# Feed-forward up-projection: 48 of 88 tile pairs as seven block products (Strassen), weights' low halves by accumulating DMA, five parts for three

## The chip, the cores and the metric

One core of one Trainium2 chip runs the whole program in one launch. The metric is device time in microseconds (us), from one run of the program; lower is better. The engines are named as in the profile: PE (TensorE, the matmuls), PEld (its weight loads), DVE (VectorE), ACT (ScalarE), POOL (GpSimd) and SP (SyncE, which here issues DMAs). Each engine works through its own list of instructions in order, and an instruction that waits for a semaphore holds up all that stands behind it in the same list.

## The reference, cut to what matters

Four layers with different token mixers; each is followed by the same kind of gated feed-forward block with a three-tap convolution along the tokens. D is 1024, D_FF is 2816, and there are 128 context tokens and 512 latent tokens, 640 in all. Modulation vectors (shift, scale, gate) come from a product of a conditioning vector with `ada_w` for each layer.

```python
def conv3_centred(x, w):
    xp = jnp.pad(x, ((0, 0), (1, 1), (0, 0)))
    return xp[:, :-2] * w[0] + xp[:, 1:-1] * w[1] + xp[:, 2:] * w[2]

def conv_ffn(h, w_up, conv_w, w_down):
    a = conv3_centred(h @ w_up, conv_w)          # h: tokens x 1024, w_up: 1024 x 5632
    g, u = a[..., :D_FF], a[..., D_FF:]
    return (jax.nn.silu(g) * u) @ w_down         # w_down: 2816 x 1024

# in reference(), for each layer l, and alike for the context tokens (xp, mod_p):
    mod_s = (jax.nn.silu(c) @ ada_w[l] + ada_b[l])[:, None, :]
    sh1s, sc1s, g1s, sh2s, sc2s, g2s = jnp.split(mod_s, 6, axis=-1)
...
    hs = modulate(xs, norm_ffn_g[l], sh2s, sc2s)
    xs = xs + g2s * conv_ffn(hs, ffn_w_up[l], ffn_conv[l], ffn_w_down[l])
```

## The kernel before

**Products.** Everything is kept feature by token: a tile has 128 features on the partitions and the 640 tokens as columns. Each f32 value is split into a high and a low part, and `mm3` makes each product as three matmuls: high by high, high by low, low by high. A matmul covers 320 columns. An up-projection tile has 8 k-tiles of 128 features, two halves of 320 columns and 3 matmuls for each, so 48 matmuls (`pe_half`, `proj`).

**The feed-forward block** (`ffn`) takes 22 pairs f of tiles for each layer: tile m = 2f is the g side, m = 2f + 1 the u side. They go in three parts of 8, 7 and 7 pairs (`PARTS`). In each part all up tiles come first ("up"), then their share of the down-projection ("dn"): 8 output tiles with 6 matmuls for each pair of the part. After the matmuls of an up tile, `post` has ACT scale it into c (L616), DVE add the two outer taps by four operations that read the PSUM tile (L618 and L620, each with 127 and with 511 columns), ACT take the silu of the g side (L633), POOL or, for the last pairs of a part, DVE multiply g by u (L640, L625), ACT cast the high part (L593) and POOL or DVE subtract for the low part (L594). dn starts on the pairs that are ready; its last needs the last pair's low part. DVE adds each dn tile into the residual x (L585).

**Weights.** SP loads a whole f32 chunk of 128x1024 into a "raw" tile; `pump1` splits it: ACT casts the high half (L86), DVE or POOL subtracts for the low half (L87). Five split tiles are kept at once.

**Modulation of the next layers** (`Ada`) is made in the shadow of the feed-forward blocks of layers 0 to 2: 144 chunks of 128x1024, a whole one at each step from a ring of tiles. For each, DVE takes a product with a sum (L209), POOL a second product (L214) and ACT the sum of that one (L215).

**Order.** The order in each engine's list is that in which the Python code calls the instructions; the waits between engines come from the tiles that they read and write, a whole tile at a time. PSUM has three double-bank tiles (`new_pair`) and two single ones.

Of the kernel before, what the change touches and what calls it, by code (L numbers as in the profile page):

```python
# [23 lines left out]
PARTS = ((0, 8), (8, 7), (15, 7))  # L24
# [27 lines left out]
class Weights:  # L52


    def __init__(self, g, chunks, slots):
        self.g, self.chunks, self.slots = g, chunks, slots
        self.loaded = self.split_n = self.used = 0
        self.raw, self.tiles = {}, {}
        self.cap = len(chunks)
        self.ahead = 2  # L60

    def load(self):
        i = self.loaded
# [12 lines left out]
    def pump1(self, pool=False):  # L76
        nc = self.g.nc
        i = self.split_n
        if i >= min(len(self.chunks), self.used + self.slots, self.cap):
            return  # L80
        while self.loaded <= i:
            self.load()
        n = self.chunks[i][1]
        raw = self.raw.pop(i)
        w = self.g.wp.tile([128, 2, 1024], F32R, tag="w", name=f"w{i}")
        nc.scalar.copy(w[:, 0, :n], raw[:, :n])  # L86
        (nc.gpsimd if pool else nc.vector).tensor_tensor(out=w[:, 1, :n], in0=raw[:, :n], in1=w[:, 0, :n], op=ALU.subtract)  # L87
        self.tiles[i] = w
        self.split_n += 1
        while self.loaded < min(self.split_n + self.ahead, len(self.chunks), self.cap):  # L90
            self.load()

    def take(self):
        while self.split_n <= self.used:
            self.pump()
        w = self.tiles.pop(self.used)
        self.used += 1
        return w


class Ada:
# [7 lines left out]
    def __init__(self, g):  # L109
# [21 lines left out]
    def micro(self):  # L131
# [15 lines left out]
        else:  # L147
            V.tensor_tensor_reduce(out=t if v else g.junk, in0=t, in1=g.cb[:, v, c], scale=1.0, scalar=0.0, op0=ALU.mult, op1=ALU.add,
# [10 lines left out]
        if self.ring is None:  # L159
            self.late.append(self.load) if self.late else self.load()  # L160

    def group(self, l, i):
# [8 lines left out]
        if self.ring is not None:  # L171
            V.memset(g.part[:, 1], 0.0)

    def open(self):

        self.ring = self.g.quad.tile([128, 5, 1024], F32, tag="quad", name=f"adaq{self.pos}")
        self.stop = len(self.queue)
        self.fresh = True
        self.pool = False
        self.hold = False  # L180
        self.flush()

    def begin(self):
        self.fresh = False
        while self.raw:
            self.micro()
        f = self.queue[self.pos][2] if self.pos < len(self.queue) else 0
        self.g.nc.vector.memset(self.g.part[:, 1, f:], 0.0)
        self.ring_load()

    def ring_load(self):
        while self.loaded < min(self.pos + 2, self.stop):
            l, i, f = self.queue[self.loaded]
            self.g.nc.sync.dma_start(out=self.ring[:, self.loaded % 3], in_=self.g.io["ada_t"][l - 1, i, f])
            self.loaded += 1

    def step(self):
        self.flush()
        if self.fresh:
            self.begin()  # L200
            return
        if self.pos >= self.stop:
            return
        g, nc = self.g, self.g.nc
        l, i, f = self.queue[self.pos]
        t, p0, p1 = self.ring[:, self.pos % 3], self.ring[:, 3], self.ring[:, 4]
        acc = g.part[:, 0, f]
        if g.mix:
            nc.vector.tensor_tensor_reduce(out=p0, in0=t, in1=g.cb[:, 0], scale=1.0, scalar=0.0, op0=ALU.mult, op1=ALU.add,  # L209
                                           accum_out=acc[:, 0:1])  # L210
        else:
            nc.gpsimd.tensor_tensor(out=p0, in0=t, in1=g.cb[:, 0], op=ALU.mult)
            self.late.append(lambda: nc.scalar.activation(p0, p0, AF.Copy, accum_out=acc[:, 0:1]))
        nc.gpsimd.tensor_tensor(out=p1, in0=t, in1=g.cb[:, 1], op=ALU.mult)  # L214
        self.late.append(lambda: nc.scalar.activation(p1, p1, AF.Copy, accum_out=acc[:, 1:2]))  # L215
        if f == KT - 1:
            self.late.append(lambda: self.group(l, i))
        self.pos += 1
        self.ring_load()

    def close(self):
        self.stop = self.loaded
        while self.pos < self.stop:
            self.step()
        self.flush()
        self.ring = None
# [1199 lines left out]
```

## Time and profile before

| | |
|---|---|
| median of 3 runs | 2717.39 us (2713.14 to 2717.69) |
| the profiled execution: own time | 2715.74 us |
| its span, first to last instruction | 2714.0 us |
| PE busy | 2675.2 us (99% of the span) |
| DVE, ACT, POOL busy | 1724.2, 1051.1, 859.0 us |
| a feed-forward part of 7 pairs, layer 1: up, then dn | 98.5 and 49.3 us |

The busy share of PE counts pipelined matmuls whose ends overlap, so a matmul's mean duration (309 ns) is longer than the distance between two. The distance is read from a stage: its length over its matmuls.

### The profile page before, as it was taken

The numbers are of one execution on the slowest core, as the hardware profiler recorded it, in microseconds if no ns is written. First come the engines' busy times: TensorE is split into PE (matmuls) and PEld (weight loads), VectorE is DVE, ScalarE is ACT, GpSimd is POOL, SyncE is SP. The second block draws the span as 40 slices with busy tenths as digits, with TensorE's granted clock in tenths as the row PEclk, the third lists the DMA queues.
The fourth block names the chain that finished last, engine by engine and source line by source line (L and its number), as shares of the span: only waits on it lengthen the run. The fifth ranks groups of instructions, "written<-read, shape, count | busy, mean of one in ns | idle before, by whom it ended". The sixth has DMA issues, their size and how long they took to land.

```text
span 2714.0 us, 45487 instructions
## 1 busy us (share of the span) xinstructions
PE 2675.2 (99%) x18950; PEld 2608.6 (96%) x18950; DVE 1724.2 (64%) x2623; ACT 1051.1 (39%) x1684; POOL 859.0 (32%) x442
## 2 busy tenths in 40 slices
PE   8999999999999999999999999999999999999998
PEld 6767999999999999999999999999999999999998
DVE  6454685868854378596866435958688548444344
ACT  4455453334442254243434224434344435223232
POOL 1223173445410144363521002635454115211121
PEclk9999999999999999999999999999999999999999
DMA  7233253334322233343322222433343123222221
GB/s 260 88 106 113 86 180 116 140 110 156 116 78 81 79 106 134 133 143 130 137 97 78 70 71 79 163 117 138 124 148 116 42 69 131 80 70 65 87 68 46
DMA packets 88335, 295.35 MB, mean 109 GB/s; under 512 B 9665, under 2 KB 15553, under 8 KB 88129
## 3 DMA queue, kind: packets, MB, share of 16 engines
q1 hardware_dynamic: 87554, 292.19, 32.0%
q8 instruction: 149, 2.44, 0.4%
q14 instruction: 56, 0.46, 0.1%
q10 hardware_dynamic: 576, 0.26, 0.0%
HBM read 289.53 MB, written 2.88 MB: 108 GB/s over the span
## 4 chain that ended last, share of the span: by engine, by line
PE 94%; DVE 2%; issue 2%; ACT 1%; DMA 0%; POOL 0%; SPq 0%; POOLq 0%; DVEq 0%; ACTq 0%
PE up L492 15%; PE up L493 15%; PE up L494 15%; PE dn L494 7%; PE dn L492 7%; PE dn L493 7%; PE sc L493 2%; PE sc L492 2%; PE sc L494 2%; PE S L774 1%; PE O L853 1%; PE qkv L492 1%; PE T L830 1%; PE sco L492 1%; PE fno L492 1%
## 5 line engine op out<-in xcount | busy, mean ns | idle before, releaser
L492 PE MATMUL up<-h,w 128*128 128x320 f32 x2816 | 871.4, 309 | 0.0
L494 PE MATMUL up<-h,w 128*128 128x320 f32 x2816 | 870.2, 309 | 0.0
L493 PE MATMUL up<-h,w 128*128 128x320 f32 x2816 | 870.1, 309 | 0.0
L87 DVE TENSOR_TENSOR w<-raw,w 128x1024 fp32r<-128x1024 f32 (+2 forms) x280 | 491.3, 1758 | 109.5 <-ACT w L86 102.0
L492 PEld LDWEIGHTS up<-h,w 128*128 128x128 f32 x2816 | 528.6, 188 | 0.3
L493 PEld LDWEIGHTS up<-h,w 128*128 128x128 f32 x2816 | 528.6, 188 | 0.3
L494 PEld LDWEIGHTS up<-h,w 128*128 128x128 f32 x2816 | 528.5, 188 | 0.0
L214 POOL TENSOR_TENSOR adaq<-adaq,cb 128x1024 f32<-128x1024 f32 x144 | 364.1, 2529 | 369.0 <-ACT adaq L215 320.2
L86 ACT CAST w<-raw 128x1024 fp32r<-128x1024 f32 (+2 forms) x361 | 363.9, 1011 | 240.3 <-PE dn L494 162.1
L492 PE MATMUL dn<-g,w 128*128 128x320 f32 x1408 | 436.3, 310 | 0.0
L494 PE MATMUL dn<-g,w 128*128 128x320 f32 x1408 | 435.1, 309 | 0.0
L493 PE MATMUL dn<-g,w 128*128 128x320 f32 x1408 | 435.1, 309 | 0.0
L87 POOL TENSOR_TENSOR w<-raw,w 128x1024 fp32r<-128x1024 f32 (+2 forms) x81 | 186.9, 2309 | 769.9 <-ACT w L86 647.6
L616 ACT ACTIVATE c<-up,fcv 128x640 f32<-128x640 f32 x176 | 140.1, 796 | 606.4 <-PE up L494 602.6
L618 DVE SCALAR_TENSOR_TENSOR c<-up,fcv,c 128x127 f32<-128x127 f32 x352 | 191.5, 544 | 230.2 <-ACT c L616 229.6
L209 DVE CUSTOM_DVE_ANT_0 adaq<-adaq,cb 128x1024 f32<-128x1024 f32 x144 | 268.8, 1867 | 0.1
L493 PEld LDWEIGHTS dn<-g,w 128*128 128x128 f32 x1408 | 264.3, 188 | 0.3
L492 PEld LDWEIGHTS dn<-g,w 128*128 128x128 f32 x1408 | 264.3, 188 | 0.3
L494 PEld LDWEIGHTS dn<-g,w 128*128 128x128 f32 x1408 | 264.3, 188 | 0.0
L585 DVE SCALAR_TENSOR_TENSOR x<-dn,mod,x 128x128 f32<-128x128 f32 (+3 forms) x204 | 99.4, 527 | 246.6 <-PE dn L494 246.5
L620 DVE SCALAR_TENSOR_TENSOR c<-up,fcv,c 128x127 f32<-128x127 f32 x352 | 193.6, 550 | 12.4
L640 POOL TENSOR_TENSOR c<-c,c 128x640 f32<-128x640 f32 x64 | 149.6, 2337 | 163.2 <-DVE c L620 158.4
(236 smaller groups left out, 3854.7 us busy)
## 6 DMA issues: line engine op xcount, KB each, us to landing
raw<-up SPq DMA_DIRECT2D x176, 512.0 KB, 4.2
adaq<-ada_t SPq DMA_DIRECT2D x144, 512.0 KB, 3.6
raw<-down SPq DMA_DIRECT2D x64, 448.0 KB, 3.9
adar<-ada SPq DMA_DIRECT2D x32, 512.0 KB, 3.6
raw<-down SPq DMA_DIRECT2D x32, 512.0 KB, 4.0
raw<-sc_in SPq DMA_DIRECT2D x24, 512.0 KB, 3.5
ada<-ada SPq DMA_DIRECT2D x16, 512.0 KB, 10.2
raw<-sgu_in SPq DMA_DIRECT2D x16, 512.0 KB, 3.6
```

Source lines behind the costliest of these rows:

```text
L86: nc.scalar.copy(w[:, 0, :n], raw[:, :n])
L87: (nc.gpsimd if pool else nc.vector).tensor_tensor(out=w[:, 1, :n], in0=raw[:, :n], in1=w[:, 0, :n], op=ALU.subtract)
L209: nc.vector.tensor_tensor_reduce(out=p0, in0=t, in1=g.cb[:, 0], scale=1.0, scalar=0.0, op0=ALU.mult, op1=ALU.add, accum_out=acc[:, 0:1])
L214: nc.gpsimd.tensor_tensor(out=p1, in0=t, in1=g.cb[:, 1], op=ALU.mult)
L492: nc.tensor.matmul(out, wh, rh, start=first, stop=False)
L493: nc.tensor.matmul(out, wh, rl, start=False, stop=False)
L494: nc.tensor.matmul(out, wl, rh, start=False, stop=last)
L585: nc.vector.scalar_tensor_tensor(out=g.x[:, m, a:b], in0=ps[:, PC0 + a:PC0 + b], scalar=gate[:, m, v:v + 1], in1=g.x[:, m, a:b], op0=ALU.m ...
L616: nc.scalar.activation(c, ps[:, PC0:PC0 + NT], AF.Copy, scale=fc[:, col + 1:col + 2])
L618: nc.vector.scalar_tensor_tensor(out=c[:, a + 1:b], in0=ps[:, PC0 + a:PC0 + b - 1], scalar=fc[:, col:col + 1], in1=c[:, a + 1:b], op0=ALU. ...
L620: nc.vector.scalar_tensor_tensor(out=c[:, a:b - 1], in0=ps[:, PC0 + a + 1:PC0 + b], scalar=fc[:, col + 2:col + 3], in1=c[:, a:b - 1], op0= ...
L640: eng.tensor_tensor(out=cg, in0=cg, in1=c, op=ALU.mult)
```

## The change

**Parts.** The 22 pairs go in five parts of 4, 4, 4, 4 and 6 pairs. In parts 1 to 4 of each layer the first three pairs (12 for each layer, 48 in all) are made by `products`, the others as before. dn is done after each part, so its 8 tiles are added to x five times instead of three.

**A pair as 2 by 2 blocks.** The blocks of the weights are (g side, u side) by (first 512 features, last 512 features); the blocks of the input are (first 512 features, last 512 features) by (first 320 tokens, last 320). Seven products of 12 matmuls (84) take the place of 96. They use seven forms of the weights: three raw blocks (A11, A12, A22) and four sums (S1 to S4), and the input halves h0, h1 with two tiles of input sums, T. The products add up in the PSUM tile X (columns X0 and X1) and in Z, and seven operations between them (L624 to L636, four copies on ACT, three additions on DVE) collect what is needed into two SBUF tiles (named C). The convolution then reads the SBUF tiles instead of PSUM (L692, L694, L696).

**Weights.** For a raw block (`sub_dma`) ACT casts the high half, ACT writes the block times -1, rounded in the same way, into the low half's place, and a DMA from POOL's queue adds the f32 block to it from memory (L97, 144 such DMAs of 256 KB). For a sum DVE forms the block (L140 to L143), then ACT casts and DVE subtracts. Tiles hold 512 columns now, eight of them at once.

**Input sums.** `sums` makes the two T tiles in part 0 of each layer, one step of six additions and two splits after each of the tiles m = 3 to 6.

**Modulation.** No ring: each 128x1024 chunk is taken as four products of 512 columns, two on DVE and two on POOL with ACT's sum. They are spread by rates: none in part 0's up, none while pairs are made by `products`, most of them in dn (5.2 products for each of the tiles at which a dn asks for them), 4.4 at each of the last up tiles of a part.

**POOL** no longer multiplies g by u or subtracts for g's low part; DVE does both for all pairs.

The diff, cut to its core:

```diff
-PARTS = ((0, 8), (8, 7), (15, 7))
+PARTS = ((0, 4), (4, 4), (8, 4), (12, 4), (16, 6))
+PAIRS = 3
...
+    FORMS = ("A11", "A12", "S2", "S1", "S3", "S4", "A22")
...
+    def sub(self, w, src, n, pool):
+        nc = self.g.nc
+        nc.scalar.copy(w[:, 0, :n], src)
+        (nc.gpsimd if pool else nc.vector).tensor_tensor(out=w[:, 1, :n], in0=src, in1=w[:, 0, :n], op=ALU.subtract)
+
+    def sub_dma(self, w, src, ap):
+        nc = self.g.nc
+        nc.scalar.copy(w[:, 0], src)
+        nc.scalar.mul(w[:, 1], src, -1.0)
+        nc.gpsimd.dma_start(out=w[:, 1], in_=ap, accum_op=ALU.add)
...
+            if name == "S2":
+                self.s1 = self.g.tmp.tile([128, 640], F32, tag="tmp", name=f"S1_{i}")
+                V.tensor_tensor(out=self.s1[:, :512], in0=ru[:, :512], in1=ru[:, 512:], op=ALU.add)
+                V.tensor_tensor(out=ru[:, :512], in0=rg[:, :512], in1=ru[:, :512], op=ALU.subtract)
+                V.tensor_tensor(out=rg[:, :512], in0=self.s1[:, :512], in1=rg[:, :512], op=ALU.subtract)
+                V.tensor_tensor(out=rg[:, 512:], in0=rg[:, 512:], in1=rg[:, :512], op=ALU.subtract)
+            src = {"S1": self.s1, "S2": rg, "S3": ru, "S4": rg}[name]
+            self.sub(w, src[:, 512:] if name == "S4" else src[:, :512], 512, False)
...
+def products(g, norm, T, X, Z, t1, t2):
...
+    def prod(f, out, b, half, first, last):
+        w = W.take_form(f)
+        for k in range(4):
+            c = slice(k * 128, (k + 1) * 128)
+            mm3(nc, out, w[:, 0, c], w[:, 1, c], b[:, k, 0, half], b[:, k, 1, half], first and k == 0, last and k == 3, not first)
+        W.pump1()
+
+    prod(0, X0, h0, lo, True, True)
+    A.copy(t1[:, lo], X0)
+    prod(1, X1, h1, lo, True, True)
+    V.tensor_tensor(out=t1[:, lo], in0=X1, in1=t1[:, lo], op=ALU.add)
+    prod(2, X0, T[1], hi, False, True)
+    A.copy(t1[:, hi], X0)
+    prod(3, Zp, T[0], lo, True, True)
+    A.copy(t2[:, hi], Zp)
+    prod(4, X0, T[0], hi, False, True)
+    V.tensor_tensor(out=t2[:, hi], in0=X0, in1=t2[:, hi], op=ALU.add)
+    prod(5, Zp, h1, hi, False, True)
+    V.tensor_tensor(out=t1[:, hi], in0=Zp, in1=t1[:, hi], op=ALU.add)
+    prod(6, X0, T[1], lo, False, True)
+    A.copy(t2[:, lo], X0)
...
+    def step(k):
+        u, v = (g.tmp.tile([128, 640], F32, tag="tmp", name=f"H{l}_{k}_{i}") for i in range(2))
+        V.tensor_tensor(out=u, in0=h0[:, k, 0], in1=h0[:, k, 1], op=ALU.add)
+        V.tensor_tensor(out=v, in0=h1[:, k, 0], in1=h1[:, k, 1], op=ALU.add)
+        V.tensor_tensor(out=u[:, a], in0=u[:, b], in1=u[:, a], op=ALU.subtract)
+        V.tensor_tensor(out=u[:, b], in0=v[:, b], in1=u[:, b], op=ALU.subtract)
+        V.tensor_tensor(out=v[:, b], in0=v[:, b], in1=u[:, a], op=ALU.subtract)
+        V.tensor_tensor(out=v[:, a], in0=v[:, a], in1=v[:, b], op=ALU.subtract)
+        split_to(g, T[0][:, k, 0], T[0][:, k, 1], u)
+        split_to(g, T[1][:, k, 0], T[1][:, k, 1], v)
...
         def post(m, ps, half):
+            conv(m, ps[:, PC0:PC0 + NT])
+            if p == 0 and 3 <= m < 7:
+                step(m - 3)
...
-                    eng = nc.gpsimd if f < f0 + nf - 2 else nc.vector
...
+        else:
+            for f in range(f0, f0 + PAIRS):
+                X, Z = new_pair(g, f"X{l}_{f}"), g.pb.tile([128, 512], F32, tag="b1", name=f"Z{l}_{f}")
+                t1, t2 = (g.tmp.tile([128, 640], F32, tag="tmp", name=f"C{l}_{f}_{i}") for i in range(2))
+                products(g, norm, T, X, Z, t1, t2)
+                conv(2 * f, t1)
+                conv(2 * f + 1, t2)
+                g.ada.flush()
+                g.W.pump1()
...
+            proj(g, f"up{l}_{p}_", 2 * (nf - PAIRS), norm.rhs, post, m0=2 * (f0 + PAIRS), rate=g.urate, quiet=1)
...
-             plan=late_plan(nf, 4), split=0, tail=3 if last else 0, norm=nxt, rate=0.0 if g.ada.ring is None else g.drate)
+             plan=late_plan(nf, nf - 1), split=0, tail=3 if last else 0, norm=nxt, rate=g.drate)
...
-    g.rate, g.urate, g.drate, g.srate, g.mix = 1.0, 1.0, 1.0, 0.0, 1
+    g.urate, g.drate, g.srate = 1.1, 1.3, 0.0
```

Two places show how the lists of the engines stand now. Rows name the line, the operation, the tile written and the tiles read.

The first place is the step from one pair to the next, in layer 1. Before, ACT's list between two up tiles of this layer (c1_18 and c1_19 are the convolution tiles of a pair, up1_1_18 is the PSUM tile of its g side, w a split weight tile, adaq a modulation chunk) reads:

```order
L616 ACTIVATE c1_18_11026<-up1_1_18_10977,fcv1_9248 128x640
L593 CAST g1_1_0_10846<-c1_16_10897 128x640
L215 ACTIVATE adaq46_9247,part_109<-adaq46_9247 128x1024
L86 CAST w148_11040<-raw148_10907 128x1024
L616 ACTIVATE c1_19_11097<-up1_1_19_11048,fcv1_9248 128x640
```

Now ACT's list from the last copy of pair 8 (X1_8 is its PSUM tile, C1_8_0 and C1_8_1 its SBUF tiles) to the first copy of pair 9 reads:

```order
L636 COPY C1_8_1_12107<-X1_8_12104 128x320
L692 ACTIVATE c1_16_12232<-C1_8_0_12106,fcv1_10147 128x640
L692 ACTIVATE c1_17_12238<-C1_8_1_12107,fcv1_10147 128x640
L703 ACTIVATE c1_16_12232<-c1_16_12232 128x640
L219 ACTIVATE ada64_12097,part_108<-ada64_12097 128x512
L95 CAST w333_12262<-raw169_12210 128x512
L96 ACTIVATE w333_12262<-raw169_12210 128x512
L624 COPY C1_9_0_12248<-X1_9_12246 128x320
```

The copy of pair 9's first product stands behind seven operations for pair 8, the modulation and a later weight form. On PE the end of pair 9's first product and the start of its second read:

```order
L505 MATMUL X1_9_12246<-h1_1_0_10068,w325_12086 128x320
L503 MATMUL X1_9_12246<-h1_1_1_10069,w326_12120 128x320 [waits Activation_49]
L504 MATMUL X1_9_12246<-h1_1_1_10069,w326_12120 128x320
L505 MATMUL X1_9_12246<-h1_1_1_10069,w326_12120 128x320 [waits DMASW1_49]
```

The second product, which writes the other half of X1_9, waits for ACT (the copy L624 of the first), and each raw block's first low-half matmul waits for its DMA from POOL's queue. The third product waits for DVE in the same way, for the addition L626. DVE's list between the two pairs reads:

```order
L696 SCALAR_TENSOR_TENSOR c1_16_12232<-C1_8_0_12106,fcv1_10147,c1_16_12232 128x511
L694 SCALAR_TENSOR_TENSOR c1_17_12238<-C1_8_1_12107,fcv1_10147,c1_17_12238 128x127
L696 SCALAR_TENSOR_TENSOR c1_17_12238<-C1_8_1_12107,fcv1_10147,c1_17_12238 128x127
L694 SCALAR_TENSOR_TENSOR c1_17_12238<-C1_8_1_12107,fcv1_10147,c1_17_12238 128x511
L696 SCALAR_TENSOR_TENSOR c1_17_12238<-C1_8_1_12107,fcv1_10147,c1_17_12238 128x511
L140 TENSOR_TENSOR S1_152_12280<-raw170_12212 128x512
L141 TENSOR_TENSOR raw170_12212<-raw169_12210,raw170_12212 128x512
L142 TENSOR_TENSOR raw169_12210<-S1_152_12280,raw169_12210 128x512
L143 TENSOR_TENSOR raw169_12210<-raw169_12210 128x512
L91 TENSOR_TENSOR w334_12279<-raw169_12210,w334_12279 128x512
L626 TENSOR_TENSOR C1_9_0_12248<-X1_9_12246,C1_9_0_12248 128x320
```

The addition of pair 9 stands behind pair 8's convolutions, the four block sums of the weights of a later pair and a low half.

The second place is dn of a part of layer 1. Before, DVE's list from one dn tile's additions into x to the next has one weight tile and one modulation product (the second row of it reads its sum):

```order
L585 SCALAR_TENSOR_TENSOR x_91<-dn1_1_3_11921,mod_106,x_91 128x128
L585 SCALAR_TENSOR_TENSOR x_91<-dn1_1_3_11921,mod_106,x_91 128x512
L87 TENSOR_TENSOR w163_11967<-raw163_11888,w163_11967 128x1024
L209 ISA adaq46_9247,part_109<-adaq46_9247,cb_89 128x1024
L209 ISA part_109 128x1
```

Now it has, for a dn tile with 24 matmuls instead of 42:

```order
L596 SCALAR_TENSOR_TENSOR x_91<-dn1_1_3_11880,mod_106,x_91 128x128
L596 SCALAR_TENSOR_TENSOR x_91<-dn1_1_3_11880,mod_106,x_91 128x512
L91 TENSOR_TENSOR w321_11909<-S1_150_11863,w321_11909 128x512
L221 ISA junk58_1_11913,part_108<-ada58_11876,cb_89 128x512
L221 ISA part_108 128x1
L221 ISA junk59_0_11918,part_108<-ada59_11916,cb_89 128x512
L221 ISA part_108 128x1
L596 SCALAR_TENSOR_TENSOR x_91<-dn1_1_4_11921,mod_106,x_91 128x128
```

In the whole of such a dn there are 16 products on DVE and 16 on POOL, each of 512 columns. In the whole program PE has 576 matmuls of 320 columns fewer; the counts of all other matmuls are the same.

## Rows read from the trace of the kernel before

**Rows 1.** The page: busy time of each engine; the chain that ended last.

```profile
PE 2675.2 (99%) x18950; PEld 2608.6 (96%) x18950; DVE 1724.2 (64%) x2623; ACT 1051.1 (39%) x1684; POOL 859.0 (32%) x442
...
PE 94%; DVE 2%; issue 2%; ACT 1%; DMA 0%; POOL 0%; SPq 0%; POOLq 0%; DVEq 0%; ACTq 0%
```

**Rows 2.** Windows: layer 1's second up and dn, then layer 3's last up.

```profile
core 0: us, PE busy (x) PEld busy (x) DVE busy (x) ACT busy (x) POOL busy (x), PEclk, DMA share, GB/s
1136.90:1235.40 98.50, 98.50 (x674) 98.50 (x673) 84.12 (x101) 43.27 (x63) 46.65 (x21) 1.00 0.39 135
1235.40:1284.70 49.30, 49.30 (x338) 49.30 (x337) 29.36 (x35) 15.46 (x21) 23.48 (x9) 1.00 0.40 138
2403.00:2501.50 98.50, 98.50 (x674) 98.50 (x673) 45.49 (x70) 30.77 (x39) 19.84 (x10) 1.00 0.21 66
```

**Rows 3.** The first of these windows, instructions on the up tiles alone (columns PE, PEld, DVE, ACT).

```profile
1136.90:1235.40 98.50, 98.47 (x672) 98.49 (x672) 27.34 (x52) 10.36 (x13) 1.00 0.39 135
```

**Rows 4.** Groups by form, whole run: operations on ACT (busy us, mean ns, idle before).

```profile
L398 ACT COPY rbc<-bc 128x320 f32<-128x320 f32 x18 | 7.6, 422 | 17.8 <-PE bc L395 17.7
L633 ACT ACTIVATE c<-c 128x640 f32<-128x640 f32 x88 | 64.1, 729 | 1.1 <-DVE c L620 1.1
L593 ACT CAST g<-c 128x640 fp32r<-128x640 f32 x88 | 63.5, 722 | 89.1 <-DVE c L640 36.6 <-DVE c L625 31.4 <-POOL c L640 21.2
L86 ACT CAST w<-raw 128x512 fp32r<-128x512 f32 x10 | 6.2, 617 | 0.0
```

**Rows 5.** Groups by form, whole run: operations on DVE and POOL.

```profile
L594 DVE TENSOR_TENSOR O<-O,O 128x512 fp32r<-128x512 f32 x10 | 6.9, 687 | 0.2 <-ACT O L593 0.2
L361 DVE TENSOR_TENSOR acc<-acc,sq 128x320 f32<-128x320 f32 x40 | 19.4, 485 | 1.6 <-ACT sq L353 1.6
L594 DVE TENSOR_TENSOR g<-c,g 128x640 fp32r<-128x640 f32 x24 | 19.8, 826 | 19.0 <-ACT g L593 19.0
L618 DVE SCALAR_TENSOR_TENSOR c<-up,fcv,c 128x127 f32<-128x127 f32 x176 | 61.0, 347 | 230.2 <-ACT c L616 229.6
L620 DVE SCALAR_TENSOR_TENSOR c<-up,fcv,c 128x511 f32<-128x511 f32 x176 | 132.0, 750 | 6.2
L585 DVE SCALAR_TENSOR_TENSOR x<-dn,mod,x 128x512 f32<-128x512 f32 x84 | 62.3, 742 | 0.0
L87 POOL TENSOR_TENSOR w<-raw,w 128x512 fp32r<-128x512 f32 x7 | 8.9, 1272 | 16.8 <-ACT w L86 16.8
```

**Rows 6.** Timeline of DVE, then of POOL, in layer 1's second up.

```profile
1196.88 2.59 DVE L87 TENSOR_TENSOR w<-raw,w 128x1024 fp32r<-128x1024 f32 x1 [0.36 <-ACT w L86]
1199.40 2.60 DVE L209 CUSTOM_DVE_ANT_0 adaq<-adaq,cb 128x1024 f32<-128x1024 f32 x1
1202.57 0.74 DVE L618 SCALAR_TENSOR_TENSOR c<-up,fcv,c 128x511 f32<-128x511 f32 x1
...
1195.99 2.40 POOL L214 TENSOR_TENSOR adaq<-adaq,cb 128x1024 f32<-128x1024 f32 x1 [4.14 <-ACT adaq L215]
1198.35 2.56 POOL L640 TENSOR_TENSOR c<-c,c 128x640 f32<-128x640 f32 x1
1201.98 1.58 POOL L594 TENSOR_TENSOR g<-c,g 128x640 fp32r<-128x640 f32 x1 [1.07 <-ACT g L593]
```

**Rows 7.** Groups by form, 2403 to 2551 us, layer 3: a weight's low half.

```profile
L87 DVE TENSOR_TENSOR w<-raw,w 128x1024 fp32r<-128x1024 f32 x14 | 17.1, 1221 | 0.5
```

**Rows 8.** Timeline, end of layer 1's second up: ACT's first and DVE's last operations.

```profile
1235.69 0.80 ACT L616 ACTIVATE c<-up,fcv 128x640 f32<-128x640 f32 x1 [1.63 <-PE up L494]
...
1240.49 0.83 DVE L594 TENSOR_TENSOR g<-c,g 128x640 fp32r<-128x640 f32 x1 [0.79 <-ACT g L593]
```

**Rows 9.** Windows around a gap of PE (columns as in Rows 2).

```profile
56.90:59.80 2.90, 0.60 (x6) 0.34 (x4) 2.56 (x5) 2.07 (x4) 0.84 (x1) 1.00 0.95 316
59.80:63.30 3.50, 3.50 (x16) 3.50 (x15) 3.50 (x2) 2.29 (x4) 3.50 (x2) 0.51 0.55 127
```

**Rows 10.** DMA issues: KB each, median us from issue to landing.

```profile
raw<-up SPq DMA_DIRECT2D x176, 512.0 KB, 4.2
```

More of the change, by code (lines that the diff above doesn't have):

```diff
@@ L74, in pump, with pump1 @@
             self.pump1(pool)
[L76 to L79, printed above, removed]
+    def pump1(self, pool=False, force=False):
+        i = self.item
+        if i >= len(self.items):
             return
[L81 to L91, printed above, removed]
+        aps, n = self.items[i]
+        pair = len(aps) == 2
+        if not force and (i >= min(self.used + self.slots, self.cap) or self.out + (1 if pair else -(-n // 512)) > self.room):
+            return
+        self.fetch(i, 0)
+        if not pair:
+            raw = self.raw.pop((i, 0))
+            ts = []
+            for c in range(0, n, 512):
+                w = self.tile()
+                self.sub(w, raw[:, c:min(c + 512, n)], min(512, n - c), pool)
+                ts.append(w)
+            self.tiles[i] = ts
+            self.item += 1
+        else:
+            self.make(i, aps)
+        self.fetch(self.item - 1, self.ahead)
@@ new lines, in make @@
+    def make(self, i, aps):
+        V = self.g.nc.vector
+        rg, ru = self.raw[(i, 0)], self.raw[(i, 1)]
+        name = self.FORMS[self.form]
+        w = self.tile()
+        if name == "A11":
+            self.tiles[i] = []
+            self.sub_dma(w, rg[:, :512], aps[0][:, :512])
+        elif name == "A12":
+            self.sub_dma(w, rg[:, 512:], aps[0][:, 512:])
+        elif name == "A22":
+            self.sub_dma(w, ru[:, 512:], aps[1][:, 512:])
+        else:
+            if name == "S2":
[6 more added lines that the diff above has]
+            self.sub(w, src[:, 512:] if name == "S4" else src[:, :512], 512, False)
+            if name == "S1":
+                self.s1 = None
+        self.tiles[i].append(w)
+        self.form += 1
+        if self.form == 7:
+            self.form = 0
+            self.raw.pop((i, 0)), self.raw.pop((i, 1))
+            self.item += 1
@@ L93, in take, with take_form @@
     def take(self):
-        while self.split_n <= self.used:
-            self.pump()
+        assert len(self.items[self.used][0]) == 1
+        while self.item <= self.used:
+            self.pump1(force=True)
         w = self.tiles.pop(self.used)
         self.used += 1
+        self.out -= len(w)
+        return w
+    def take_form(self, f):
+        i = self.used
+        while self.item == i and self.form <= f:
+            self.pump1(force=True)
+        w = self.tiles[i][f]
+        self.out -= 1
+        if f == 6:
+            self.tiles.pop(i)
+            self.used += 1
@@ L147, in micro @@
         else:
-            V.tensor_tensor_reduce(out=t if v else g.junk, in0=t, in1=g.cb[:, v, c], scale=1.0, scalar=0.0, op0=ALU.mult, op1=ALU.add,
+            V.tensor_tensor_reduce(out=t if v else g.tmp.tile([128, 640], F32, tag="tmp", name=f"junk{self.pos}_{a}")[:, :512], in0=t, in1=g.cb[:, v, c], scale=1.0, scalar=0.0, op0=ALU.mult, op1=ALU.add,
                                    accum_out=acc)
@@ L170, in group @@
         self.done.add((l, i))
[L171 to L226, printed above, removed]
     def flush(self):
```

154 lines of the change are left out of this document (87 added, 67 removed).

## The prediction

> **What bounds the kernel now.** I read the page first. PE is busy for 2675.2 of 2714.0 us and makes 94% of the chain that ended last; DVE has 64%, ACT 39%, POOL 32% [rows 1]. So the kernel is bound by PE, nearly without gaps, and a matmul that goes away is worth its distance to the next one. For that distance I went to the windows of single stages: layer 1's second up lasts 98.5 us at a granted clock of 1.00, its dn 49.3 us, and layer 3's last up, without modulation work, again 98.5 [rows 2]. The up tiles of the first window are 672 matmuls in 98.47 us [rows 3], so 0.1465 us for each 320 columns. The other engines do not set these lengths: DVE is busy for 84.12 us in layer 1's up and for 45.49 us in layer 3's, with the same 98.5 [rows 2]. But 84 of 98.5 says that DVE has little to spare when its work grows and PE's shrinks.
>
> **What the change removes.** 576 matmuls x 0.1465 = 84.4 us, if PE keeps its pace. The count is exact, by the lists. The other terms are waits of PE that the lists now contain.
>
> **Prices.** ACT: copy of 320 columns 0.42, 640 columns 0.73, cast of 512 columns 0.62 [rows 4]. DVE: 320 columns 0.49, 512 columns 0.69, 640 columns 0.83; reading PSUM, 127 columns 0.35, 511 and 512 columns 0.75 [rows 5]. The tap additions on SBUF tiles do not occur in the trace. With 511 columns I take 0.69. With 127 columns the bounds are 0.35 (the PSUM form) and 0.28 (the line through 0.485 at 320 and 0.826 at 640 columns, drawn on to 127); I take 0.29. Four of them, one tile's convolution, are then 1.95 us. A POOL product of 512 columns takes 1.27 [rows 5]. Hops between engines are a few hundredths: ACT's L616 starts at 1235.69, right behind the up's end in the windows at 1235.40 plus the run-out of the last matmul [rows 2, 8]. They are left out.
>
> **Waits between the pairs.** PE may start a pair's second product only after ACT's copy of the first, and the third only after DVE's addition. A product lasts 12 x 0.1465 = 1.76 us, so that is all the cover there is. First pair of a part: copy 0.42, addition 0.49, and hops: 1.0 us. From the first to the second pair, counted from the last matmul of the first: ACT copies (0.42), scales (0.73, to 1.15); DVE's four taps run to 3.1; ACT's silu, which waits for them, to 3.85; the cast and the multiplication of a later weight form to 5.1; only now the copy, to 5.5. PE has used 1.76 of it: 3.75 us of waiting. DVE meanwhile does the second convolution (to 5.05), four weight sums (2.75, to 7.8), a low half (to 8.5) and the addition (to 9.0), while the second product ended at 7.26: 1.7 more, 5.5 in all. From the second to the third pair, ACT's list has the cast of g as well, which waits for DVE's multiplication: copy and scaling to 1.15, taps to 3.1, multiplication to 3.9, cast to 4.65, the second scaling to 5.4, silu to 6.1, two casts to 7.35, copy to 7.8: 6.0 of waiting, and 0.5 at the addition. Sum for a part: 1.0 + 5.5 + 6.5 = 13.0 us, and 16 parts have it: **+208**. Below: half of it, if prices on SBUF tiles are far lower. Nothing at all is excluded, since each step waits for the one ahead of it.
>
> **dn's lead.** The last pair's g is ready 5.6 us after its up's end: from ACT's 1235.69 to the end of DVE's last operation, 1240.49 + 0.83 [rows 8]. With four pairs, dn's plan has 3 x 3 x 3 = 27 matmuls that need no last pair: 3.96 us. In parts 1 to 3 of four layers that leaves 12 x 1.7 = **+20**. Before, the plan had 36 (5.3 us) and more behind them. Part 4 has 45 (6.6 us) and waits for nothing.
>
> **Input sums.** In part 0, at each of four up tiles DVE has four taps (2.2), two low halves (1.38), and a step of four operations of 640 and four of 320 columns (5.26): 8.8 us; two of the four tiles add a multiplication and g's low half (1.65). That is 38.6 against PE's 4 x 48 x 0.1465 = 28.1, so DVE falls 10.5 us behind. Tile m = 7 wins back 1.8 (5.2 against 7.0), and the last pair's chain adds the 1.7 of above: dn starts 10.4 us late, four times: **+42** (0, if DVE's backlog were absorbed by dn's first tiles, to 56).
>
> **Modulation in dn.** A dn of four pairs lasts 192 x 0.1465 = 28.1 us. DVE's work in it, alone: 16 products of 0.69 (11.0), eight additions into x of 1.1 (8.7), some twelve weight operations of 0.69 (8.3): 28.0, as much as PE's. POOL's 16 products of 1.27 take 20.3, 72% of the time. What happens when both run is in the timeline: POOL's product from 1195.99 to 1198.39, DVE's L87 from 1196.88 for 2.59; POOL's next from 1198.35 to 1200.91, DVE's L209 from 1199.40 for 2.60; but L618, which reads PSUM, takes 0.74 beside POOL's L594 [rows 6]. Without modulation work the same L87 takes 1.22 [rows 7]. So a DVE operation with two SBUF inputs and a POOL product take turns, each waiting for the other's whole instruction. The Trainium skill ("SBUF — State Buffer", section on the two separate sides) calls this an exclusive lock on a port pair held for the full instruction; by that rule, too, the loser waits. From the rows: a DVE operation meets a product with 72% and waits for half of it, 0.46 us; 28 such operations make 12.8 us of backlog at dn's end, which the next pair's additions wait for. Some of it hides in waits that the pairs have anyway: I take 12, between 0 (all hidden) and 24 (strict turns, 16 x 1.96 = 31 us beside 17 of other work). It applies to four dn of three layers: 12 x 12 = **+144** (0 to 288).
>
> **The clock.** After a gap, in which PE was busy for 0.60 of 2.90 us, the granted clock fell to 0.51 for 3.5 us [rows 9], which is the level of 1.2 instead of 2.4 GHz and costs half of that, 1.7. There are 48 new gaps of over 3 us (32 between pairs, 12 + 4 around dn): 0 to 82 us. I take half: **+40**.
>
> **Sum**, against the profiled execution's own time of 2715.74 (within 0.1% of the median 2717.39): 2715.7 - 84.4 + 208 + 20 + 42 + 144 + 40 = **3085 us**. The weights cost nothing in it: cast, multiplication, a POOL product ahead and 4.2 us to landing [rows 10] make some 6.7 us, and forms are made seven products ahead, 12.3 us. Without that cover, see rival D.
>
> **Rivals.**
> A. *The waits are hidden; the removed matmuls show*: 2715.7 - 84 = 2631. It needs the waits of a part to stay under 84.4 / 16 = 5.3 us. For it speaks that all of the work on ACT is short; against it, that ACT's list puts two whole convolution steps of one pair ahead of the next one's copy. Chance 0.06; the zone of no change, within 0.2%, adds 0.02.
> B. *Only the chains cost; the modulation hides under them and the clock stays up*: 2715.7 - 84.4 + 270 = 2901. For it: DVE's backlog and ACT's chain run at the same time, and a wait is paid once. Against it: backlog at a part's start comes before the chain. Chance 0.27.
> C. *Half of the chains*, because operations on SBUF tiles or short forms are quicker than their nearest rows: 2715.7 - 84.4 + 135 = 2766. Chance 0.11.
> D. *Low halves come late.* PE's first low-half matmul of each raw block waits for a DMA from POOL's list, which stands behind products that wait for DVE. No such DMA is in the trace before. At 3 us for each of 48 pairs: 3085 + 144 = 3229. The Trainium skill ("SBUF — State Buffer", section on the two sides, "DVE blocks DMA") says that descriptors of such DMAs wait while DVE holds the port; no run here shows it, and another of its pages ("DMA: Bandwidth & Descriptors", anatomy of a DMA from GpSimd) would make 2.6 us of 256 KB, an estimate by its fit, which the lead covers. Chance 0.06.
>
> **The numbers.** The sum as worked out has 0.48, with a range of its own of 2940 (modulation and clock both near nothing) to 3270 (both at their upper ends, less what they share). 0.2% is about what a measurement of this kernel can tell from no change. Faster 0.06, same 0.02, slower 0.92. The range for 8 in 10 goes from 2800, which leaves out A and half of C, to 3270, which leaves out most of D.
>
> **What would show it.** In the profile after: PE's idle time on the X tiles with ACT's L624 (3 to 6 us) and DVE's L626 as releasers; 10 us on dn's matmuls in part 0; DVE's L221 at over 1 us instead of 0.69, and a late first pair behind dn of layers 0 to 2 but not of layer 3; granted clocks of 0.5 behind the gaps. It is wrong if X's idle time is under 5 us for a part, if layer 3's parts take as long as layer 1's (no cost of the modulation), or if low-half matmuls wait on DMAs.

## The result and the profile after

The changed kernel takes 3455.74 us (median of 4 runs, 3442.5 to 3461.57) against 2715.3 for the kernel before: ratio 1.272, 95% interval 1.268 to 1.276. It is 740 us slower; the prediction was 3085 us, 370 slower, with a range from 2800 to 3270.

The page of the changed kernel answers to [rows 1]: busy times, then the slices with the granted clock in tenths, then the chain that ended last.

```profile
PE 2821.0 (82%) x18374; PEld 2702.2 (78%) x18374; DVE 2050.7 (59%) x3934; ACT 1393.4 (40%) x2835; POOL 748.2 (22%) x628
...
PEclk9999888888999988888899999787898899799989
...
PE 34%; DVE 12%; issue 6%; ACT 5%; POOL 3%; DMA 2%; DVEq 0%; POOLq 0%; ACTq 0%
```

PE is on the chain for 34% instead of 94%: no single engine bounds the kernel now. PE has 576 matmuls fewer and is busy for 146 us more, at a mean clock of 0.893 instead of 0.997. What PE waits for, in the whole run (line waited for, total us, times, longest):

```profile
PE X L503 <- ACT C L624: 356.6, 48, 18.1
PE dn L503 <- DVE c L696: 71.2, 19, 6.5
PE X L503 <- DVE C L626: 57.9, 48, 5.4
PE dn L503 <- DVE x L596: 56.1, 11, 12.4
PE X L503 <- DVE x L596: 21.8, 11, 3.5
PE dn L503 <- ACT g L604: 14.7, 4, 4.5
```

The largest is at the place foreseen, the copy of a pair's first product (L624), 48 times. Its size was not foreseen: some 180 of the 356.6 us stand at the first pair of the twelve parts of layers 0 to 2, 12 to 18 us each, where the prediction had 1.0 for copy, addition and hops together. No row has a matmul waiting for the accumulating DMA (L97). By stage, windows as in [rows 2]: one part of layer 1 (up, dn), one of layer 3 (up, dn), dn of part 0 of layer 3.

```profile
1294.50:1384.20 89.70, 58.96 (x350) 57.08 (x350) 54.27 (x93) 39.09 (x78) 19.00 (x17) 0.83 0.39 96
1384.20:1417.80 33.60, 30.00 (x193) 29.52 (x192) 21.18 (x45) 11.88 (x26) 12.66 (x10) 0.95 0.48 141
2993.90:3066.30 72.40, 60.14 (x350) 58.28 (x349) 41.62 (x71) 29.91 (x53) 4.35 (x5) 0.86 0.30 67
3066.30:3096.30 30.00, 28.91 (x194) 28.19 (x193) 17.04 (x30) 10.00 (x17) 3.48 (x4) 1.00 0.47 130
2937.80:2993.90 56.10, 34.14 (x194) 33.04 (x193) 38.35 (x66) 19.90 (x41) 16.42 (x12) 0.76 0.43 126
```

An up with three pairs needs 348 x 0.1465 = 51.0 us of PE. Layer 3, with no modulation, takes 72.4, layer 1 takes 89.7; in both, PE is busy for longer than 51, at a clock of 0.83 to 0.86. To keep waits and clock apart I took the starts of successive matmuls in the feed-forward blocks: what a distance over 0.62 us has above 0.1465 counts as a wait, what a shorter one has as slow pace. The column "time" goes from the first matmul's start to the last one's, summed over the layers, and "PE's need" is the count of matmuls by 0.1465.

| us, four feed-forward blocks | time | PE's need | waits | slow pace |
|---|---|---|---|---|
| before | 1870 | 1856 | 7 | 7 |
| changed | 2602 | 1772 | 636 | 195 |
| changed, no modulation products | 2218 | 1772 | 296 | 150 |
| all mends (see Experiments), no modulation products | 1974 | 1772 | 146 | 57 |
| five parts alone | 1900 | 1856 | 31 | 13 |

So the 742 us between the two profiled executions are -84 of matmuls, some +628 of waits, +188 of slow pace and some 10 outside the feed-forward blocks. The modulation makes 385 us in these blocks, the difference of the second and third rows: 340 of waits and 45 of slow pace. By place, 222 of them stand in the ups with pairs, 115 in the dns behind them and 45 in dn of part 0.

### The profile page after: what moved, and what is told of

Its sections match the earlier page's. It is cut to its first block, busy times and chain, and to the rows that moved or that the text cites. A ratio compares the mean times of both kernels' runs of the same rounds, so it can differ in the third digit from the quotient of the medians.

```text
span 3456.2 us, 47947 instructions
## 1 busy us (share of the span) xinstructions
PE 2821.0 (82%) x18374; PEld 2702.2 (78%) x18374; DVE 2050.7 (59%) x3934; ACT 1393.4 (40%) x2835; POOL 748.2 (22%) x628
## 4 chain that ended last, share of the span: by engine, by line
PE 34%; DVE 12%; issue 6%; ACT 5%; POOL 3%; DMA 2%; DVEq 0%; POOLq 0%; ACTq 0%
PE X L503 3%; POOL ada L218 3%; PE X L505 3%; PE X L504 3%; DMA ada<-ada_t 2%; DVE junk L221 2%; PE up L505 2%; PE up L503 2%; PE up L504 2%; PE dn L504 2%; PE dn L503 2%; PE dn L505 2%; DVE c L696 2%; PE sc L505 2%; PE sc L503 2%
## 5 line engine op out<-in xcount | busy, mean ns | idle before, releaser
L218 POOL TENSOR_TENSOR ada<-ada,cb 128x512 f32<-128x512 f32 x288 | 435.9, 1552 | 834.7 <-DVE part L221 818.7
L91 DVE TENSOR_TENSOR w<-raw,w 128x512 fp32r<-128x512 f32 (+1 forms) x557 | 362.8, 679 | 354.6 <-ACT w L90 354.5
L90 ACT CAST w<-raw 128x512 fp32r<-128x512 f32 (+1 forms) x664 | 380.9, 606 | 246.3 <-DVE raw L142 158.9
L503 PE MATMUL X<-h,w 128*128 128x320 f32 x384 | 156.5, 408 | 378.4 <-ACT C L624 356.6
L503 PE MATMUL up<-h,w 128*128 128x320 f32 x1280 | 401.5, 314 | 8.2 <-ACT w L90 8.2
L505 PE MATMUL up<-h,w 128*128 128x320 f32 x1280 | 400.0, 313 | 0.5 <-DVE w L91 0.5
L504 PE MATMUL up<-h,w 128*128 128x320 f32 x1280 | 399.4, 312 | 0.0
L221 DVE CUSTOM_DVE_ANT_0 junk<-ada,cb 128x512 f32<-128x512 f32 x288 | 266.3, 962 | 89.0 <-DMA ada<-ada_t 88.6
L97 POOL DMA_DIRECT2D w<-up x144 | 127.0, 884 | 848.7 <-ACT w L96 806.6
L219 ACT ACTIVATE ada<-ada 128x512 f32<-128x512 f32 x288 | 180.6, 627 | 289.6 <-POOL ada L218 289.0
L91 POOL TENSOR_TENSOR w<-raw,w 128x512 fp32r<-128x512 f32 (+1 forms) x107 | 138.0, 1310 | 595.0 <-ACT w L90 579.9
L503 PEld LDWEIGHTS up<-h,w 128*128 128x128 f32 x1280 | 244.5, 191 | 9.6 <-ACT w L90 9.3
L505 PEld LDWEIGHTS up<-h,w 128*128 128x128 f32 x1280 | 244.1, 191 | 1.6 <-DVE w L91 1.6
L503 PE MATMUL X<-T,w 128*128 128x320 f32 x576 | 197.6, 343 | 57.9 <-DVE C L626 57.9
L504 PEld LDWEIGHTS up<-h,w 128*128 128x128 f32 x1280 | 244.4, 191 | 0.3
```

The source lines that it names most:

```text
L90: nc.scalar.copy(w[:, 0, :n], src)
L97: nc.gpsimd.dma_start(out=w[:, 1], in_=ap, accum_op=ALU.add)
L218: g.nc.gpsimd.tensor_tensor(out=o, in0=t, in1=g.cb[:, v, c], op=ALU.mult)
L219: self.late.append(lambda: g.nc.scalar.activation(o, o, AF.Copy, accum_out=acc))
L221: V.tensor_tensor_reduce(out=t if v else g.tmp.tile([128, 640], F32, tag="tmp", name=f"junk{self.pos}_{a}")[:, :512], in0=t, in1=g.cb[:, v ...
L503: nc.tensor.matmul(out, wh, rh, start=first, stop=False, skip_group_check=more)
```

## Experiments

Each time is that of one run, beside the kernel before at 2713 to 2715 us on the same chip. The four runs of the changed kernel lie up to 19 us apart, so differences of 20 to 30 us between single runs say little.

**The modulation left out.** Edit, in the function that issues one product, and a memset of its sums:

```diff
-        if self.pool is True or (self.pool and v):
+        if True:
+            pass
+        elif self.pool is True or (self.pool and v):
```

> Leaves out the modulation's products in the feed-forward blocks (DVE's, POOL's and ACT's sums), keeps their loads and everything else. Theory 1 (the modulation's chain DVE, POOL, ACT, DMA holds up the pairs of layers 0 to 2 and dn of part 0): a layer's five parts take 675 us in layer 1 and 568 in layer 3 now; without the products all layers come to layer 3's time less some 14 us of part 0's dn, so 3456 - 3 x 107 - 3 x 14 = about 3090 us. Rival (the waits are those of the pairs' own chain and the modulation hides under it): 3400 or more.

Measured 3078.4 us, 377 less. Layer 1's first part with pairs is now like layer 3's (windows of layer 1's up and dn, layer 3's up):

```profile
1166.60:1236.60 70.00, 57.76 (x350) 56.05 (x350) 41.78 (x73) 29.92 (x53) 4.32 (x5) 0.88 0.40 105
1236.60:1266.70 30.10, 29.00 (x194) 28.27 (x194) 17.18 (x31) 9.99 (x17) 3.45 (x4) 1.00 0.76 242
2614.00:2683.90 69.90, 57.64 (x350) 55.92 (x349) 41.65 (x71) 29.93 (x53) 4.35 (x5) 0.88 0.30 69
```

Theory 1 holds. What stays without modulation is the prediction's other terms: 13.4 to 14.6 us of waits in an up with pairs, 1.5 in its dn, some 10 in dn of part 0.

**The second product in Z.**

```diff
-    X0, X1, Zp = X[:, 192:512], X[:, 512:832], Z[:, :320]
+    X0, X1, Zp = X[:, 192:512], Z[:, :320], Z[:, :320]
```

> The second product of a pair goes into the Z tile instead of X's other half, so it need not wait for the copy of the first, and the third not for the addition. Theory 1 (the order of ACT's and DVE's lists makes the waits; PE's cover is one product): the cover becomes two products, the waits at the copies of the second and third pair get 1.8 us shorter each and the first's 0.5 shorter: 16 x 4 = 64 us less, about 3390. Rival (the waits have to do with the matmuls' weights or inputs): no change, 3456.

Measured 3334.7, 121 less: about twice what was expected. Waits in layer 3's ups with pairs fall from 13.6 to 7.3 us a part, 6.3 instead of the 4 expected, and slow pace from some 7 to 4.0: about a third of the gain there is the clock, which the expectation had left out.

**Deferred convolutions.**

```diff
+    mid(0)   # behind the addition of product 1: conv of the pair before, g side
...
+    mid(1)   # behind the addition of product 4: its u side
...
-                conv(2 * f, t1)
-                conv(2 * f + 1, t2)
+                prev = [(2 * f, t1), (2 * f + 1, t2)]
...
+            for q in prev:
+                conv(*q)
```

> The convolution of a pair is issued inside the next pair's products (after the second and the fifth product), the last pair's right behind it; one weight tile fewer, one temporary tile more. Theory 1 (order of the lists): the copies are no longer behind the convolutions, the waits between pairs go (13.6 us a part in layer 3, and with them 6 us at half the clock): layer 3's parts come to 82 to 86 us from 102, the whole to about 3456 - 16 x 19 = 3150. Theory 2 (DVE has too much work, whatever the order): the waits move to other places, 3350 to 3450.

Measured 3238.0, 218 less where some 300 were expected. Windows of the same up in layers 1 and 3:

```profile
1233.00:1309.40 76.40, 56.61 (x350) 54.37 (x349) 49.79 (x91) 38.47 (x78) 19.34 (x16) 0.87 0.41 106
2825.30:2883.50 58.20, 53.12 (x350) 51.01 (x349) 40.59 (x70) 29.76 (x54) 5.18 (x6) 1.00 0.40 92
```

Layer 3's part came to 88 us (expected 82 to 86), its clock to 1.00: seven waits of 0.7 to 1.7 us instead of two long ones, 6.1 us in all, slow pace 1.2. Theory 1 holds for the pairs' own chain. Layer 1 keeps 18 us over layer 3, as it had 17 without the mend, so the mend does not touch the modulation; the expected total had not allowed for that.

**No accumulating DMA.**

```diff
-        nc.scalar.mul(w[:, 1], src, -1.0)
-        nc.gpsimd.dma_start(out=w[:, 1], in_=ap, accum_op=ALU.add)
+        nc.vector.tensor_tensor(out=w[:, 1], in0=src, in1=w[:, 0], op=ALU.subtract)
```

> The low halves of raw blocks by a DVE subtraction, as the sums' are, in place of ACT's multiplication and the accumulating DMA. Theory 1 (the DMAs land in time; no matmul waits for them in the trace): nothing gained there; DVE has 144 x 0.69 = 99 us more, ACT 90 less: 3440 to 3530. Rival D of the prediction (late low halves, or POOL's list held up by them) : faster by over 50 us, under 3400.

Measured 3480.5, 25 more. Rival D falls: the DMAs are not what PE waits for. What their issue costs in POOL's list stays open, since the edit also gives DVE more work (busy for 2131.4 us instead of 2050.7): the waits at L624 are 30 us shorter in this run (326.8), those at L626 40 us longer (97.9).

**All mends, no modulation.** The two mends above, and the input sums spread:

```diff
-            if p == 0 and 3 <= m < 7:
-                step(m - 3)
+            if p == 0 and m in (4, 6):
+                step(m // 2 - 2)
...
+            if p == 0 and m in (3, 5):      # in dn of part 0
+                step(m // 2 + 1)
```

> All mends together and no modulation products (left out as before): deferred convolutions, the second product in Z, and the input sums spread, one at each of the up tiles m = 4 and 6 and two in dn of part 0. Theory 1 (lists' order, modulation and the half clock behind each gap explain the loss, the removed matmuls are worth their 84 us): 3078 less 16 x 17 for the pairs with their slow clock and 4 x 11 for part 0, about 2760, and the granted clock back to 0.98. Theory 2 (DVE's or ACT's sheer work in these parts bounds them even without the modulation): no better than 2900.

Measured 2836.2, clock 0.979. Theory 2 (2900) is out, but 2760 was not reached: waits of 1.4 us at the third product's copy and 4.9 in dn of part 0 stay, among others. With the modulation kept, the same mends:

> All three mends with the modulation kept: deferred convolutions, the second product in Z, the input sums spread over two up tiles and dn of part 0. From the deferred run, 3238, less about 4 us a part for the second product and 8 to 10 us for each of four part 0: 3130 to 3160, still slower than before, since the modulation's 240 to 370 us stay. Rival (the mends hide most of the modulation too): under 3000.

Measured 3207.3: 371 over the run without it, and above the 3130 to 3160 expected. The two mends added to the deferred convolutions gave 31 us here, and the mends hide none of the modulation.

**The next weight form behind the copy.** In the kernel of 2836, `W.pump1()` moves from the matmuls' end to behind each copy or addition.

> As the run with all mends and no modulation (2836), with the next weight form issued behind the copy or addition of a product instead of ahead of it. If the 65 us of waits at the copy of the third product (46 times 1.4 us) come from the casts ahead of it in ACT's list: 2750 to 2780. If they come from the copy's own wait for DVE's addition into the same SBUF tile: 2820 to 2840.

Measured 2818.6, just under the second range: of the 65 us of waits at this copy 33 remain, in 16 waits, but the whole gains only 18. A part's up with three pairs (layer 3) is then:

```profile
2414.80:2471.70 56.90, 53.49 (x351) 52.59 (x350) 44.52 (x79) 32.67 (x60) 6.12 (x7) 0.97 0.42 98
```

**Five parts alone**, in the kernel before:

```diff
-PARTS = ((0, 8), (8, 7), (15, 7))
+PARTS = ((0, 4), (4, 4), (8, 4), (12, 4), (16, 6))
...
-plan=late_plan(nf, 4)
+plan=late_plan(nf, min(4, nf - 1))
```

> The kernel before with five parts and nothing else (dn's lead takes one k-tile fewer than the part's pairs where there are four). Expected from dn's lead alone: 16 x 1.7 = 27 us more, 2742, and nothing from the additional additions into x, since DVE has room. If parts are what costs: 2800 or more.

Measured 2748.1, 33 more where 27 were expected, so parts are not what costs.

**The changed kernel without pairs by products** (`PAIRS = 0`, no input sums), with its modulation, without it, and with it spread (`urate` 1.0, `drate` 0.6):

> The changed kernel without its pairs by seven products and without input sums: all pairs as before, but five parts, weights in halves, the modulation without a ring and g's work on DVE. If the loss of the modulation needs the pairs' short cover, these layers run with few waits: 2740 to 2780. If the modulation's chain (products behind loads one at a time, in dn) holds up PE by itself: 2850 to 2950.

> The changed kernel without pairs by seven products, without input sums and without the modulation's products (left out). If the 186 us over five parts alone come from the modulation: 2750 to 2775. If they come from the weights in halves or g's work on DVE: 2850 or more.

> The changed kernel without pairs and input sums, the modulation kept but spread: 4 products for each up tile and 2.4 for each dn tile instead of 4.4 and 5.2. If its density in dn makes the waits: 2770 to 2830. If every product costs, wherever it stands: 2900 to 2950.

Measured 2934.1 (the second range), 2780.0 (5 us over the first) and 2886.1 (between the two). A layer 1 part of the first (up, dn) and of the second (up, dn):

```profile
1152.20:1212.70 60.50, 57.56 (x392) 57.22 (x391) 41.42 (x86) 29.37 (x68) 28.91 (x20) 1.00 0.46 140
1212.70:1259.00 46.30, 32.50 (x193) 31.34 (x194) 26.90 (x59) 16.23 (x37) 19.05 (x14) 0.78 0.42 136
...
1166.30:1222.60 56.30, 56.30 (x386) 56.30 (x385) 30.30 (x54) 16.87 (x27) 0.00 (x0) 1.00 0.43 134
1222.60:1252.60 30.00, 28.97 (x194) 28.25 (x194) 14.69 (x28) 8.06 (x13) 2.88 (x2) 1.00 0.63 211
```

By itself the modulation costs 154 us in this form, most of it in dn, 46.3 us instead of 30.0 here, where the up has 60.5 instead of 56.3. Spread it costs 106. (In the first run the rates finish it within two layers, since there are more up tiles that ask for it.) So the same modulation costs 377 beside the pairs and 154 without them. The second run lies 32 us over five parts alone; no run takes apart which of the remaining changes, weights in halves and g's work on DVE among them, makes that.

**Which half of the modulation.** Each run leaves out one half, in the same function as above.

> The changed kernel without POOL's half of the modulation (POOL's products and ACT's sums of them left out; DVE's products and all loads stay). Theory 1 (the link that holds up the pairs is ACT's list: its sums wait for POOL's products, and the copies that PE waits for stand behind them): nearly all of the 377 us that leaving out everything gave, 3090 to 3160. Theory 2 (DVE's load and its 288 products): about half or less, 3250 to 3350.

> The changed kernel without DVE's half of the modulation (POOL's products, ACT's sums and all loads stay). Theory 1 (ACT's list behind POOL): POOL still takes 1.27 us a product, each sum still waits for one, so less than half of the 377: 3270 to 3400. Theory 2 (DVE): 3090 to 3200. If POOL and DVE hold each other up by turns, both of these runs give more than half.

Measured 3204.7 without POOL's half (251 less, between the two ranges) and 3284.6 without DVE's (171 less, in the range of theory 1). The sum is 422, against 377 for both, so neither engine is the cause alone, and each of them counts; turns by themselves do not explain it, as only one of the two runs gives more than half. Without POOL, DVE's product takes 0.70 us on the mean, with it 0.96.

Where PE waits tells more: at the copy of a pair's first product, then at the addition of its second, without POOL's half, without DVE's, and without both (where the two lines are L626 and L628).

```profile
PE X L503 <- ACT C L624: 170.2, 48, 5.9
PE X L503 <- DVE C L626: 102.4, 48, 8.2
...
PE X L503 <- ACT C L624: 305.4, 48, 14.2
PE X L503 <- DVE C L626: 40.9, 48, 3.3
...
PE X L505 <- ACT C L626: 164.9, 48, 5.9
PE X L505 <- DVE C L628: 35.0, 48, 1.2
```

With the whole modulation the copy had 356.6. Nearly all that the modulation adds there, 192 us, goes with POOL's products and ACT's sums of them, and 141 us of it stay without DVE's products. With DVE's half alone the wait stands at the addition instead, 67 us more than with neither half: that is the backlog of DVE that the prediction had in mind, and it is the smaller of the two.

**Loads two ahead** (`self.loaded > self.pos + 1`):

> The changed kernel with the modulation's chunks loaded two ahead instead of one. DVE waits 88.6 us for these loads in all. If they are a link of the chain that holds up the pairs: 40 to 90 us less, with the half clock behind it, 3370 to 3415. If the chain is only the turns of DVE and POOL and the waits between lists: within 15 us of 3456.

Measured 3420.1, 36 less, a little short of the range for a link. DVE's waits for these loads fall from 88.6 to 26.7 us, but the waits at L624 stay (354.5 against 356.6): what is gained stands in dn, and the loads are not what holds up the copy.

**The modulation spread over the pairs**, in the kernel with all mends (DVE's product also goes into a small tile of its own):

```diff
+    g.ada.filler(0.25)     # behind each copy or addition of a pair
...
+    g.urate, g.drate, g.srate = 0.5, 0.75, 0.0
```

> The run with all mends and the modulation kept (3207), with the modulation spread: one product behind each of a pair's block products, 2 for each up tile, 3 for each dn tile. If its density in dn makes the waits: 2950 to 3050. If, in the pairs, DVE and POOL have no room for it either, since each pair waits for its additions and copies within two products: 3150 to 3350.

Measured 3181.0, 26 less than 3207. The waits move from dn into the pairs: at the first product's copy they fall from 167.5 to 93.3 us, at the third product's they rise from 81.6 to 132.0. The second theory fits.

## Why the prediction was wrong

**The removed matmuls.** 84 us, right: PE's need fell from 1856 to 1772, and between the waits the matmuls kept the distance of 0.1465 us where the clock was 1.00.

**Waits between the pairs.** 13.0 us a part was right, 13.4 to 14.6 measured where no modulation is in the way. The chain can be read in layer 3, ACT from the last copy of a pair to the first of the next, then PE's start behind it:

```profile
3008.23 0.43 ACT L636 COPY C<-X 128x320 f32<-128x320 f32 x1 [0.56 <-PE X L505]
3008.55 1.55 ACT L692 ACTIVATE c<-C,fcv 128x640 f32<-128x640 f32 x2
3011.70 0.74 ACT L703 ACTIVATE c<-c 128x640 f32<-128x640 f32 x1 [1.60 <-DVE c L696]
3012.35 0.60 ACT L95 CAST w<-raw 128x512 fp32r<-128x512 f32 x1
3012.86 0.62 ACT L96 ACTIVATE w<-raw 128x512 fp32r<-128x512 f32 x1
3013.39 0.40 ACT L624 COPY C<-X 128x320 f32<-128x320 f32 x1
...
3013.84 0.64 PE L503 MATMUL X<-h,w 128*128 128x320 f32 x1 [3.89 <-ACT C L624]
```

3.75 us of waiting was predicted, 3.89 came, and 5.91 for the 6.0 of the next pair. The taps on SBUF tiles took 0.35 and 0.75 us, not 0.29 and 0.69. In part the sum is luck: the second pair's addition kept PE waiting for 0.58 us and not 1.7, as PE made the product before it at half the clock, and the first pair's waits were some 1.5 us and not 1.0.

**dn's lead and input sums.** Without modulation dn waits 1.5 us in parts 1 to 3 (1.7 predicted) and some 10 in part 0 (10.4). In the changed kernel part 0's dn waits for up to 23 us in layers 1 to 3: `need(l, 5)` then forces what is left of the modulation in front of dn's first additions (12.4 us, the largest wait for L596 above). The prediction had not counted that; it is most of the 45 us of modulation in dn of part 0.

**The modulation: the step that failed.** 144 us (0 to 288) was predicted, 377 measured, of which some 45 are slow pace. (By its own numbers, strict turns give 31 + 17 - 28 = 20 us a dn and not 24, so the upper end was some 240.) The prediction counted work and turns of DVE and POOL, and let DVE's backlog hold up the next pair's additions. The turns are there (0.96 us for L221 instead of 0.70), and so is the backlog at the addition, but the path that it left out, ACT's sums ahead of the copy, is the longer one. Layer 1, the end of a dn whose last matmul was at 1417.6 us, first DVE, then POOL, then ACT, then PE:

```profile
1426.35 0.82 DVE L221 CUSTOM_DVE_ANT_0 junk<-ada,cb 128x512 f32<-128x512 f32 x1
1431.02 1.65 DVE L221 CUSTOM_DVE_ANT_0 junk<-ada,cb 128x512 f32<-128x512 f32 x1 [3.84 <-DMA ada<-ada_t]
1432.60 1.00 DVE L596 SCALAR_TENSOR_TENSOR x<-dn,mod,x 128x128 f32<-128x128 f32 x2
...
1432.75 1.27 POOL L218 TENSOR_TENSOR ada<-ada,cb 128x512 f32<-128x512 f32 x1 [0.65 <-DVE part L221]
1436.11 0.87 POOL L97 DMA_DIRECT2D w<-up  x1 [2.09 <-ACT w L96]
1436.72 1.56 POOL L218 TENSOR_TENSOR ada<-ada,cb 128x512 f32<-128x512 f32 x1
...
1430.92 0.63 ACT L219 ACTIVATE ada<-ada 128x512 f32<-128x512 f32 x1 [2.51 <-POOL ada L218]
1438.31 0.63 ACT L219 ACTIVATE ada<-ada 128x512 f32<-128x512 f32 x1 [2.50 <-POOL ada L218]
...
1439.98 0.40 ACT L624 COPY C<-X 128x320 f32<-128x320 f32 x1
...
1440.43 0.64 PE L503 MATMUL X<-h,w 128*128 128x320 f32 x1 [17.17 <-ACT C L624]
```

ACT's sums wait for POOL's products. POOL's products write in place over what DVE still reads, and stand behind the issue of a DMA (L97) that waits for ACT. DVE waits here for a chunk that is loaded when the one ahead is done. The copy that frees PE stands behind the last sum and two operations on a weight in ACT's list. Every engine is idle in turns, and the pair's second product starts 17 us late. That POOL's half with ACT's sums is what holds up the copy, the runs with half of the modulation show (170.2 and 305.4 us); that it is the order in ACT's list is read from the rows, as no run changed that order alone. Dividing load by time cannot show this; ACT's list of the changed kernel, followed from the sums to the copy, has it. What part of the 377 each link has was not settled: the halves give 251 and 171, the loads 36, another spread 26 to 48, and they overlap.

**The clock: the other step that failed, as a term mis-sized.** +40 (0 to 82) predicted, 188 measured. Granted clock in windows behind that gap of 3.89 us:

```profile
3009.90:3013.80 3.90, 0.05 (x1) 0.00 (x0) 3.79 (x8) 2.29 (x5) 0.07 (x2) 0.80 0.86 130
3013.80:3021.40 7.60, 6.98 (x25) 6.58 (x26) 4.36 (x7) 1.24 (x2) 0.84 (x1) 0.50 0.22 36
3026.00:3029.00 3.00, 3.00 (x22) 3.00 (x22) 0.56 (x2) 0.73 (x2) 0.86 (x1) 1.00 0.70 171
```

PE stays at 0.50, the level of 1.2 GHz, for 7.6 us, twice the 3.5 of [rows 9]; a second wait of 0.58 us lies in it. So this gap costs some 3.5 us and not 1.7. There were also more gaps: 77 distances of over 3 us where 48 were counted (40 without modulation), and the clock fell to 0.50 at all of them, where half had been taken. The mean is 188 / 77 = 2.4 us. Some 45 of the 188 are the modulation's and stand in its 377 too.

**Rivals.** B, with the modulation hidden, is near what the run without modulation shows, plus the clock: 2901 + 143 of added slow pace = 3044, 3078 measured. D fell with its run. A would need more than the mends gave: with no modulation, all mends and the weight forms behind the copies, an up of three pairs by products and one ordinary pair takes 54.2 to 56.9 us, and one of four ordinary pairs 56.3. The seven products cost PE in short waits most of what they spare it, the input sums and the five parts come on top, and no version tried is faster than the kernel before.

## What to carry to other kernels

When PE is 99% busy, its matmuls cover waits of other engines that no row shows. Before cutting its work, follow in each other engine's list what stands ahead of the operation that frees PE's next accumulation, to the end of the chain. Seven products for eight need a copy or an addition out of PSUM behind every product; here even the version with convolutions and weight forms moved behind the copies, and no modulation, did not win (2818.6). Count a gap of PE at its length plus what the lower clock costs behind it, and do not put background work whose links span three engines and a load into a list where a short wait counts.

## What the runs showed of the hardware

An accumulating DMA from POOL's queue holds POOL for 0.88 us and lands 256 KB in 4.8 us, where SP's loads land 512 KB in 3.6:

```profile
L97 POOL DMA_DIRECT2D w<-up x144 | 127.0, 884 | 848.7 <-ACT w L96 806.6 <-DVE c L696 18.7 <-DVE S L140 16.8
...
raw<-up SPq DMA_DIRECT2D x176, 512.0 KB, 3.6
w<-up POOLq DMA_DIRECT2D x144, 256.0 KB, 4.8
```

The estimate from the Trainium skill ("DMA: Bandwidth & Descriptors", anatomy of a DMA from GpSimd) for 256 KB was 2.6 us; the measurement, 4.8 for these accumulating DMAs, decides. A DVE tap with two SBUF inputs takes as long as one from PSUM (0.745 and 0.741 us for 511 columns). After a gap of 3.89 us the granted clock stayed at 0.50 for 7.6 us, with a gap of 0.58 in them; after the gap of [rows 9] it did for 3.5. With seven gaps of 0.7 to 1.7 us in one up (58.2 us) of the run with deferred convolutions it stayed at 1.00.
